# Layer 0's second shift on VectorE in the last two branches, the scale alone on TensorE, and the gate's row behind two row tiles of the output projection

## The chip, the cores and the metric

The kernel runs on one core of one Trainium2 chip. Its engines are TensorE (PE in the rows; PEld is its weight load), VectorE (DVE), ScalarE (ACT), GpSimd (POOL) and SyncE (SP, which here issues nearly all DMAs). The metric is the device time of one execution in microseconds (us), as the median of several runs, lower being better.

## The reference, cut to what matters

One inference step of a two-layer network over 256 latent and 128 context tokens, D = 1024. Each layer is a token-mixing sub-layer and a channel mixer, both wrapped in a modulation and a gate that depend on two condition vectors, one for each token group (v = 0 context, v = 1 latent):

```python
sh1, sc1, g1, sh2, sc2, g2 = split(silu(c) @ w_mod[l] + b_mod[l], 6)
h = layer_norm(x) * (1 + sc1) + sh1
...  # attention, convolution and Fourier branches, merged by three sigmoid gates
x = layer_norm(ALPHA * x + g1 * (merged @ w_o)) * ln1_g + ln1_b
h = layer_norm(x) * (1 + sc2) + sh2
...  # up projection, depthwise conv of 3, silu gate, down projection
x = layer_norm(ALPHA * x + g2 * (... @ w_down)) * ln2_g + ln2_b
```

The six vectors of 1024 that `w_mod` gives are read by the kernel in three pairs: "A" is (sh1, sc1), "B" is (sh2, sc2), "G" is (g1, g2), with j = 0 or 1 for the member of the pair. The change deals with where B of layer 0 is computed, and with when g1 is made ready for use.

## The kernel before

**Products.** Activations are kept transposed (features on partitions, 384 tokens in the free dimension). Each weight tile of 128x1024 is split into a high part (`whi`, a cast on ScalarE, L183) and a low part (`wlo`, a subtraction on VectorE, L184); each product is then three matmuls (`mm3`, L200, L201, L202). The pools are small: 3 `raw` tiles of 1 MB, 5 `whi`, 5 `wlo`, 8 `s4` tiles of 512 KB, 8 `s2` tiles of 256 KB, and in PSUM 2 `ps` and 6 `acc` tiles.

**Token mixing** (`mixing`, L624) computes the projections, then three branches in turn, each over eight 128-row tiles m: Fourier (branch 0, with the attention's `scores` and `values` and the depthwise convolution `conv_branch` spread over it), attention output (branch 1) and convolution output (branch 2). For each m a branch does a gate product of 24 matmuls (L666), tanh on ScalarE (L669), an output product (12 matmuls in branch 1, 6 in branches 0 and 2), a merge on VectorE (L683) and an addition on GpSimd (L684). In branch 2 the merged tile is split again for the next product (`split`, ScalarE L652, VectorE L653).

**The attention's values** (`values`, L873): for each head of a pair, seven transposes, a ScalarE copy of 512 columns (L884) and a VectorE copy of 384 columns (L885) from PSUM, then the products L893 and L896.

**Modulation has two ways.** On TensorE, `mod_stream` (L252) brings 8 tiles of 512 columns a step (two k of four quarters each, `STRIDE` = 2), multiplies them in `mod_products` (L221, 32 rows of PSUM a quarter), and after the last k `mod_columns` copies the sums, transposes them in four blocks (L301) and adds the bias. Before, layer 0 does the whole pair B so, in four steps; each instruction of L221 shows as two records in the trace, so the 32 instructions of the pair are 64 records. On VectorE, `mod_rows` (L311) multiplies a row-major 512 KB tile of `w_modr` by a broadcast condition vector and sums along the row, for both v (L331, two instructions for a tile, eight tiles for one vector of 1024, called a unit here). `paced` (L357) spreads the units' tiles over a number of calls: before, in each layer's mixing one unit (g1) over 10 calls, from tile m = 4 of branch 1 on.

**The gate's row** (`gate_rows`, L346): the unit's sums are transposed on TensorE (L351), copied by ScalarE (L353) and written to a scratch in HBM (L354), from which `gate_bc` (L370) reads them back to all partitions, 512 KB for each v. Before, this stands at the end of `mixing` (L736); `layer` (L971) then asks for the gate and the layer norm's vectors and starts the output projection, four loads of `w_o` with two row tiles k each. The first three k are multiplied for all tokens, the last five (`TAIL`) token tile by token tile, so that the closing of tile 0 (`close`, L943 on) can begin early. `close` multiplies each half by the gate first.

**Order.** The program text gives the order of priorities; the framework fixes each engine's queue when it builds, so an instruction can stand ahead of its place in the text, but each queue then runs strictly in that order. `issue_after` pins an instruction behind a given one.

Of the kernel before, what the change touches and what calls it, by code (L numbers as in the profile page):

```python
# [77 lines left out]
class Net:  # L78
# [135 lines left out]
    STRIDE = 2  # L214
# [37 lines left out]
    def mod_stream(self, groups):  # L252


        steps = [(l, kind, k) for l, kind in groups for k in range(0, KD, self.STRIDE)]
        src = {}

        def fetch(l, kind, k0):
            for k in range(k0, k0 + self.STRIDE):
                w = self.a["w_mod"][l, self.MODS[kind], k].rearrange("p j (i c) -> p (j i) c", c=512)  # L260
                for i in range(4):
                    src[k, i] = self.s2()
                    self.load(src[k, i], w[:, i])

        fetch(*steps[0])
        yield
        for n, (l, kind, k0) in enumerate(steps):
            if k0 == 0:
                ps = self.psum("acc")
            self.mod_products(ps, src, range(k0, k0 + self.STRIDE), 512)  # L270
            if k0 + self.STRIDE == KD:
                if kind == "G":
                    self.mod_gates(l, ps)
                else:
                    self.mod_columns(l, kind, ps, 512, 0, "acc")
            if n + 1 < len(steps):
                fetch(*steps[n + 1])
            yield

    def mod_gates(self, l, ps):  # L280
        nc, a, n = self.nc, self.a, 512
        row = self.s2()
        nc.gpsimd.memset(row, 0.0)
        r4 = row.rearrange("(j i r) c -> j i r c", r=32, j=2)
        for v in range(2):
            for j in range(2):
                self.load(r4[j, :, v, :], a["b_g"][l, j].rearrange("(i c) -> i c", c=n))
        nc.vector.tensor_tensor(row, ps, row, op=ALU.add)
        for v in range(2):
            for j in range(2):  # L290
                nc.sync.dma_start(self.gscr[l, j, v].rearrange("(i c) -> i c", c=n), r4[j, :, v, :])
# [54 lines left out]
    def gate_rows(self, tag):  # L346

        nc = self.nc
        for l, j, cols in self.gate_sums:
            pt = self.psum(tag)[0:2 * KD, 0:P]  # L350
            nc.tensor.transpose(pt, cols, self.ident)  # L351
            row = self.kk()[0:2 * KD, :]
            nc.scalar.copy(row, pt)  # L353
            nc.sync.dma_start(self.gscr[l, j].rearrange("v (k p) -> (v k) p", p=P), row)  # L354
        self.gate_sums = []
# [268 lines left out]
    def mixing(self, l, first, hT, mods, rows):  # L624
# [69 lines left out]
        mods = self.mod_stream(mods) if mods else iter(())  # L694
# [4 lines left out]
        step_rows = self.paced(rows, 10)  # L699
# [24 lines left out]
        for i, _ in enumerate(branch(1, 0, "w_a", 4, aT, lambda: values(3))):  # L724
            next(cb, None)
            if i >= 4:
                step_rows()
            if i % 2:
                mod()
# [6 lines left out]
        self.gate_rows("acc")  # L736
# [77 lines left out]
    def attention(self, l, z, cv, out):  # L814
# [58 lines left out]
        def values(j):  # L873
            pT = []
            for par in range(2):
# [9 lines left out]
                nc.vector.tensor_copy(p[:, 512:896], pts[1][:, 0:384])  # L885
# [85 lines left out]
    def layer(self, l, first, hT, mods, mix_rows, rows):  # L971
        nc, a = self.nc, self.a
        m_hl = self.mixing(l, first, hT, mods, mix_rows)
        gate = self.gate_bc(l, 0)
        lg, lb = self.bcast(a["ln"][l, 0]), self.bcast(a["ln"][l, 1])
# [3 lines left out]
        for u in range(KD // 2):  # L979
            for h, w in enumerate(self.row_halves(self.raw(a["w_o"][l, u]))):  # L980
                k = 2 * u + h
                if k < KD - self.TAIL:
                    self.x_mm(acc, k, KD, m_hl[k], w, range(3), off)
                else:
                    held.append((k, w))

# [146 lines left out]
    def run(self):  # L1133
        self.setup()
        xhat = [self.s4() for _ in range(3)]
        mods = [[(0, "B")], []]
        mix_rows = [[(0, "G", 0)], [(1, "G", 0)]]
# [83 lines left out]
```

## Time and profile before

| | |
|---|---|
| median of 3 runs | 1136.67 us (1135.53 to 1137.31) |
| the profiled execution | 1136.51 us, of which the span is 1134.6 us |
| granted TensorE clock | 0.998 of full speed |
| TensorE / VectorE / ScalarE / GpSimd busy | 98% / 78% / 46% / 8% |

Layer 0's mixing runs from about 60 to 254 us of the span, its output projection to 273 us; layer 1's mixing ends at 804 us. Branch 0 is under way at 100 us in layer 0 and at 657 us in layer 1. The rows below are taken from the profile's page and from views of the trace.

### The profile page before, as it was taken

What the parts mean: (1) busy time and instruction counts of PE and PEld (TensorE: products, weight loads), DVE (VectorE), ACT (ScalarE), POOL (GpSimd) and SP (SyncE); (2) the same over time, 40 slices, a digit from 0 to 9 for tenths busy, and PEclk for the clock granted to TensorE, in tenths of its full rate; (3) what the DMA queues carried; (4) which work ended last, traced back from release to release, by engine and by line L of the source; (5) the groups of instructions that cost most, each with busy time, mean ns of one, the idle gap of its engine ahead of it and who ended that gap; (6) DMA issues with size and microseconds to landing.
All of it is one profiled execution on the core that took longest, in us unless ns stands there. A gap on an engine that the chain in (4) does not pass through costs nothing.

```text
span 1134.6 us, 16426 instructions
## 1 busy us (share of the span) xinstructions
PE 1116.2 (98%) x6385; PEld 1014.7 (89%) x6385; DVE 888.2 (78%) x1519; ACT 521.8 (46%) x879; POOL 89.5 (8%) x89
## 2 busy tenths in 40 slices
PE   9999999999999999999999999999999999999996
PEld 7788889998999998999957989999889999999995
DVE  6579968856899999999776699796579975556668
ACT  3457744342754343443363686334356343444440
POOL 1010003221100000000011000222120000000001
PEclk9999999999999999999999999999999999999999
DMA  9863563636566666658335222564626543434511
GB/s 377 309 214 130 168 240 117 218 111 223 186 223 222 217 212 217 238 177 294 113 112 185 96 75 75 191 217 149 231 92 253 194 141 117 144 111 158 176 38 55
DMA packets 41821, 199.04 MB, mean 175 GB/s; under 512 B 4912, under 2 KB 6032, under 8 KB 26640
## 3 DMA queue, kind: packets, MB, share of 16 engines
q1 hardware_dynamic: 41312, 197.21, 49.8%
q8 instruction: 50, 0.82, 0.3%
q10 hardware_dynamic: 432, 0.79, 0.2%
q14 instruction: 27, 0.22, 0.1%
HBM read 194.53 MB, written 3.45 MB: 174 GB/s over the span
## 4 chain that ended last, share of the span: by engine, by line
PE 83%; DVE 10%; ACT 2%; issue 2%; POOL 1%; DMA 1%; POOLq 0%; DVEq 0%; ACTq 0%
PE ps L200 16%; PE ps L202 16%; PE ps L201 16%; PE acc L200 9%; PE acc L201 9%; PE acc L202 9%; DVE wlo L184 1%; PE acc L893 1%; DVE s L331 1%; DVE sm L425 1%; DVE s L944 1%; POOL sm L429 1%; PE acc L129 1%; PE acc L881 1%; DMA s<-w_modr 1%
## 5 line engine op out<-in xcount | busy, mean ns | idle before, releaser
L184 DVE TENSOR_TENSOR wlo<-raw,whi 128x1024 fp32r<-128x1024 f32 x216 | 269.4, 1252 | 145.1 <-ACT whi L183 141.2
L200 PE MATMUL ps<-hT,whi 128*128 128x386 f32 (+1 forms) x1088 | 370.3, 340 | 2.4 <-ACT g L669 1.5
L202 PE MATMUL ps<-hT,wlo 128*128 128x386 f32 (+1 forms) x1088 | 368.9, 339 | 0.0
L201 PE MATMUL ps<-hT,whi 128*128 128x386 f32 (+1 forms) x1088 | 368.6, 339 | 0.0
L183 ACT CAST whi<-raw 128x1024 fp32r<-128x1024 f32 x216 | 225.9, 1050 | 309.8 <-PE ps L201 183.0
L200 PEld LDWEIGHTS ps<-hT,whi 128*128 128x128 f32 x1088 | 205.3, 189 | 9.0 <-issue 3.3
L201 PEld LDWEIGHTS ps<-hT,whi 128*128 128x128 f32 x1088 | 205.4, 189 | 1.5 <-issue 0.4
L202 PEld LDWEIGHTS ps<-hT,wlo 128*128 128x128 f32 x1088 | 205.5, 189 | 0.8 <-issue 0.7
L331 DVE SCALAR_TENSOR_TENSOR s<-s,s 128x1024 f32<-128x1024 f32 x128 | 160.8, 1256 | 5.0 <-DMA s<-w_modr 4.5
L201 PE MATMUL acc<-wlo,r 128*128 128x512 f32 x360 | 142.4, 396 | 0.9 <-DVE wlo L184 0.9
L202 PE MATMUL acc<-whi,r 128*128 128x512 f32 x360 | 141.9, 394 | 0.0
L200 PE MATMUL acc<-whi,r 128*128 128x512 f32 x360 | 140.4, 395 | 0.0
L202 PEld LDWEIGHTS acc<-whi,r 128*128 128x128 f32 x360 | 67.7, 188 | 15.8 <-DVE r L1077 0.5
L201 PEld LDWEIGHTS acc<-wlo,r 128*128 128x128 f32 x360 | 67.7, 188 | 15.5 <-DVE wlo L184 1.3
L200 PEld LDWEIGHTS acc<-whi,r 128*128 128x128 f32 x360 | 67.7, 188 | 14.7
L429 POOL TENSOR_TENSOR sm<-sm,mhalf 128x1 f32<-128x1 f32 x21 | 26.8, 1274 | 625.2 <-DVE sm L428 625.2
L911 DVE SCALAR_TENSOR_TENSOR cv<-upad,cst,cv 128x399 f32<-128x399 f32 x120 | 70.6, 633 | 0.1
L684 POOL TENSOR_TENSOR g<-g,g 128x384 f32<-128x384 f32 x32 | 45.1, 1409 | 322.6 <-DVE g L683 322.6
L1053 ACT ACTIVATE g<-ps,cst 128x386 f32<-128x386 f32 x84 | 56.1, 667 | 0.0
L1054 DVE SCALAR_TENSOR_TENSOR g<-ps,cst,g 128x385 f32<-128x385 f32 x84 | 51.6, 614 | 2.5 <-ACT g L1053 2.4
L1056 DVE SCALAR_TENSOR_TENSOR g<-ps,cst,g 128x385 f32<-128x385 f32 x84 | 51.9, 618 | 1.3
L1076 ACT CAST r<-g 128x386 fp32r<-128x386 f32 x44 | 22.6, 514 | 65.8 <-DVE g L1074 65.8
(194 smaller groups left out, 1318.5 us busy)
## 6 DMA issues: line engine op xcount, KB each, us to landing
raw<-w_u SPq DMA_DIRECT2D x44, 1024.0 KB, 4.9
s<-w_modr SPq DMA_DIRECT2D x64, 512.0 KB, 3.6
raw<-w_g SPq DMA_DIRECT2D x24, 1024.0 KB, 5.0
raw<-w_d SPq DMA_DIRECT2D x22, 1024.0 KB, 4.9
raw<-w_mod SPq DMA_DIRECT2D x8, 1024.0 KB, 8.6
s<-w_mod SPq DMA_DIRECT2D x32, 256.0 KB, 4.6
raw<-w_o SPq DMA_DIRECT2D x8, 1024.0 KB, 4.9
s<-w_z SPq DMA_DIRECT2D x8, 512.0 KB, 9.8
```

Of the source, the lines that this page charges most:

```text
L183: self.nc.scalar.copy(hi, raw)
L184: self.nc.vector.tensor_tensor(lo, raw, f32(hi), op=ALU.subtract)
L200: mm(ps, lh, rh, start=first, stop=False)
L201: mm(ps, lh, rl, start=False, stop=False)
L202: self.last_mm = mm(ps, ll, rh, start=False, stop=last)
L331: nc.vector.scalar_tensor_tensor(prod, w[i % 2], 1.0, cb[v], op0=ALU.mult, op1=ALU.mult, accum_out=sums[n][:, v * KD + k:v * KD + k + 1])
L429: nc.gpsimd.tensor_tensor(mv[:, 3:4], mv[:, 2:3], self.mhalf, op=ALU.pow)
L684: nc.gpsimd.tensor_tensor(merged[m], merged[m], gt, op=ALU.add)
L911: nc.vector.scalar_tensor_tensor(c, u[:, i:i + CV_W], w, c, op0=ALU.mult, op1=ALU.add)
L1053: nc.scalar.activation(c, ps, AF.Identity, bias=cols["ffn_b"][:, i:i + 1], scale=w[1])
L1054: nc.vector.scalar_tensor_tensor(c[:, 1:NPAD], ps[:, 0:NPAD - 1], w[0], c[:, 1:NPAD], op0=ALU.mult, op1=ALU.add)
L1056: nc.vector.scalar_tensor_tensor(c[:, 0:NPAD - 1], ps[:, 1:NPAD], w[2], c[:, 0:NPAD - 1], op0=ALU.mult, op1=ALU.add)
```

## The change

`mod_stream` now computes only the scale of B (j = 1), for the layer it is given; `mod_columns` stays for nothing but what the first projection does by itself. A step takes four k (`STRIDE` = 4) of 1024 columns: again 8 tiles of 512 columns, each of which holds two quarters of 256, so there are two steps and 32 instructions of 256 columns; `mod_column` makes two transposes, not four. The shift of B (j = 0) becomes a unit of layer 0's mixing beside g1, so there are two units there, over 14 calls from tile m = 2 of branch 1 on. Layer 1 keeps one unit over 10 calls. The VectorE copy in `values` goes to ScalarE in both layers. `gate_rows` moves, in both layers, from the end of `mixing` to behind the first load of the output projection (two k), takes a `ps` tile instead of an `acc` tile, and its transpose is pinned behind the last matmul of those two k; the loads of the gate and the layer norm's vectors stand behind all of `w_o`'s in the text. `mod_gates`, which nothing called, is gone.

```diff
-    STRIDE = 2
+    STRIDE = 4
...
-    def mod_stream(self, groups):
-        steps = [(l, kind, k) for l, kind in groups for k in range(0, KD, self.STRIDE)]
+    def mod_stream(self, l):
         src = {}
-        def fetch(l, kind, k0):
+        def fetch(k0):
             for k in range(k0, k0 + self.STRIDE):
-                w = self.a["w_mod"][l, self.MODS[kind], k].rearrange("p j (i c) -> p (j i) c", c=512)
-                for i in range(4):
-                    src[k, i] = self.s2()
-                    self.load(src[k, i], w[:, i])
+                w = self.a["w_mod"][l, self.MODS["B"], k, :, 1]
+                for h in range(2):
+                    t = self.s2()
+                    self.load(t, w[:, h * 512:h * 512 + 512])
+                    for i in range(2):
+                        src[k, 2 * h + i] = t[:, i * 256:i * 256 + 256]
...
-            self.mod_products(ps, src, range(k0, k0 + self.STRIDE), 512)
+            self.mod_products(ps, src, range(k0, k0 + self.STRIDE), 256)
...
+    def mod_column(self, l, j, ps):
+        nc = self.nc
+        row = self.s2()[:, 0:256]
+        nc.vector.tensor_copy(row, ps[:, 0:256])
+        pt = self.psum("acc")
+        for q in range(2):
+            nc.tensor.transpose(pt[:, q * P:(q + 1) * P], row[:, q * P:(q + 1) * P], self.ident)
+        bias = self.bmod[l][:, j + 3, :].rearrange("p (i q) -> p i q", q=2)
         for v in range(2):
+            part = pt[:, 0:256].rearrange("p (q i r) -> p r i q", q=2, i=4)[:, v]
+            dst = self.modcol[l][:, j + 2, v, :].rearrange("p (i q) -> p i q", q=2)
+            nc.vector.tensor_tensor(dst, part, bias, op=ALU.add)
...
-    def gate_rows(self, tag):
+    def gate_rows(self, tag, after=None):
...
-            nc.tensor.transpose(pt, cols, self.ident)
+            if after:
+                with self.tc.issue_after(after):
+                    nc.tensor.transpose(pt, cols, self.ident)
+            else:
+                nc.tensor.transpose(pt, cols, self.ident)
...
-        step_rows = self.paced(rows, 10)
+        step_rows = self.paced(rows, 14 if len(rows) > 1 else 10)
...
-            if i >= 4:
+            if i >= (2 if len(rows) > 1 else 4):
                 step_rows()
...
-        self.gate_rows("acc")
         return m_hl
...
-                nc.vector.tensor_copy(p[:, 512:896], pts[1][:, 0:384])
+                nc.scalar.copy(p[:, 512:896], pts[1][:, 0:384])
...
         m_hl = self.mixing(l, first, hT, mods, mix_rows)
-        gate = self.gate_bc(l, 0)
-        lg, lb = self.bcast(a["ln"][l, 0]), self.bcast(a["ln"][l, 1])
...
+            if u == 0:
+                self.gate_rows("ps", self.last_mm.ins)
+        gate = self.gate_bc(l, 0)
+        lg, lb = self.bcast(a["ln"][l, 0]), self.bcast(a["ln"][l, 1])
...
-        mods = [[(0, "B")], []]
-        mix_rows = [[(0, "G", 0)], [(1, "G", 0)]]
+        mods = [True, False]
+        mix_rows = [[(0, "B", 0), (0, "G", 0)], [(1, "G", 0)]]
```

## Rows read from the trace of the kernel before

**Rows 1.** Page, part 1; stages: length, engines (PE to POOL), clock, DMA share, GB/s.

```profile
PE 1116.2 (98%) x6385; PEld 1014.7 (89%) x6385; DVE 888.2 (78%) x1519; ACT 521.8 (46%) x879; POOL 89.5 (8%) x89
...
103.00:157.00 54.00, 54.00 (x352) 44.24 (x351) 50.85 (x113) 36.14 (x88) 0.00 (x0) 1.00 0.54 184
...
165.00:182.00 17.00, 17.00 (x101) 16.96 (x100) 8.55 (x16) 4.17 (x6) 3.56 (x4) 1.00 0.42 157
182.00:222.00 40.00, 40.00 (x232) 39.82 (x231) 37.33 (x57) 15.34 (x21) 12.63 (x7) 1.00 0.56 184
222.00:255.00 33.00, 33.00 (x190) 32.74 (x188) 17.41 (x25) 15.29 (x24) 8.20 (x7) 1.00 0.39 128
255.00:270.00 15.00, 15.00 (x66) 12.20 (x65) 7.33 (x9) 4.23 (x5) 1.20 (x1) 1.00 0.87 311
```

**Rows 2.** The chain of waits, modulation products (start, us, what).

```profile
43.46 1.88 PE ps L221 x64
...
118.95 1.85 PE acc L221 x16
...
157.52 0.44 PE acc L301 x4
```

**Rows 3.** The same columns, between the same instructions of layers 0 and 1.

```profile
100.19:179.11 78.92, 78.89 (x501) 67.21 (x502) 63.87 (x137) 45.93 (x103) 2.04 (x2) 1.00 0.57 197
657.26:729.19 71.93, 71.93 (x433) 65.48 (x434) 63.74 (x132) 45.84 (x103) 2.94 (x2) 1.00 0.36 128
```

**Rows 4.** Groups of instructions by line: copies, row sums; weight loads' waits.

```profile
L331 DVE SCALAR_TENSOR_TENSOR s<-s,s 128x1024 f32<-128x1024 f32 x128 | 160.8, 1256 | 5.0 <-DMA s<-w_modr 4.5
L884 ACT COPY s<-acc 128x512 f32<-128x512 f32 x16 | 8.9, 579 | 2.5 <-PE acc L881 2.5
L885 DVE COPY s<-acc 128x384 f32<-128x384 f32 x16 | 8.8, 552 | 3.0 <-PE acc L882 2.8
L761 ACT COPY g<-acc 128x256 f32<-128x256 f32 x8 | 3.4, 428 | 0.0
...
PEld acc L893 <- ACT s L884: 2.4, 7, 0.8
PEld acc L893 <- DVE s L885: 1.1, 2, 0.8
```

**Rows 5.** The last two branches in order of time, on VectorE, TensorE and GpSimd.

```profile
218.12 1.22 DVE L184 TENSOR_TENSOR wlo<-raw,whi 128x1024 fp32r<-128x1024 f32 x1
219.25 2.04 DVE L331 SCALAR_TENSOR_TENSOR s<-s,s 128x1024 f32<-128x1024 f32 x1
...
222.56 0.55 DVE L683 SCALAR_TENSOR_TENSOR g<-g,acc 128x384 f32<-128x384 f32 x1
...
226.92 0.55 DVE L683 SCALAR_TENSOR_TENSOR g<-g,acc 128x384 f32<-128x384 f32 x1
...
230.34 1.22 DVE L184 TENSOR_TENSOR wlo<-raw,whi 128x1024 fp32r<-128x1024 f32 x1 [2.40 <-ACT whi L183]
...
217.01 0.34 PE L202 MATMUL acc<-r,wlo 128*128 128x384 f32 x1
...
222.27 0.34 PE L202 MATMUL acc<-r,wlo 128*128 128x384 f32 x1
...
227.61 1.20 POOL L684 TENSOR_TENSOR g<-g,g 128x384 f32<-128x384 f32 x1 [3.36 <-DVE g L683]
```

**Rows 6.** The gate's row and the first closing in order of time; its DMAs.

```profile
253.96 0.27 PE L351 MATMUL acc<-ident,sm 128*16 128x128 f32 x1
...
254.62 0.33 SPq L354 DMA_DIRECT2D gscr<-kk  x1
...
256.71 0.80 SPq L122 DMA_DIRECT2D s<-gscr  x2
...
270.27 0.69 DVE L943 TENSOR_TENSOR s<-acc,s 128x512 f32<-128x512 f32 x1 [1.18 <-PE acc L202]
...
DMA to landing us min/median/max: 2.0/7.2/8.1
```

More of the change, by code (lines that the diff above doesn't have):

```diff
@@ L250, in mod_first @@
         yield
-    def mod_stream(self, groups):
-        steps = [(l, kind, k) for l, kind in groups for k in range(0, KD, self.STRIDE)]
+    def mod_stream(self, l):
         src = {}
-        def fetch(l, kind, k0):
+        def fetch(k0):
             for k in range(k0, k0 + self.STRIDE):
-                w = self.a["w_mod"][l, self.MODS[kind], k].rearrange("p j (i c) -> p (j i) c", c=512)
-                for i in range(4):
-                    src[k, i] = self.s2()
-                    self.load(src[k, i], w[:, i])
-        fetch(*steps[0])
+                w = self.a["w_mod"][l, self.MODS["B"], k, :, 1]
[4 more added lines that the diff above has]
+                        src[k, 2 * h + i] = t[:, i * 256:i * 256 + 256]
+        fetch(0)
@@ L266, in mod_stream @@
         yield
-        for n, (l, kind, k0) in enumerate(steps):
+        for k0 in range(0, KD, self.STRIDE):
             if k0 == 0:
                 ps = self.psum("acc")
-            self.mod_products(ps, src, range(k0, k0 + self.STRIDE), 512)
+            self.mod_products(ps, src, range(k0, k0 + self.STRIDE), 256)
             if k0 + self.STRIDE == KD:
[L272 to L277, printed above, removed]
-            yield
@@ L280, in mod_gates @@
[L280 to L284, printed above, removed]
-        for v in range(2):
[L286 to L291, printed above, removed]
+                self.mod_column(l, 1, ps)
+            else:
+                fetch(k0 + self.STRIDE)
@@ L350, in gate_rows @@
             pt = self.psum(tag)[0:2 * KD, 0:P]
-            nc.tensor.transpose(pt, cols, self.ident)
+            if after:
+                with self.tc.issue_after(after):
+                    nc.tensor.transpose(pt, cols, self.ident)
+            else:
+                nc.tensor.transpose(pt, cols, self.ident)
             row = self.kk()[0:2 * KD, :]
@@ L693, in mixing @@
             self.columns(l + 1, self.columns_load(l + 1), nc.vector.tensor_copy)()
-        mods = self.mod_stream(mods) if mods else iter(())
+        mods = self.mod_stream(l) if mods else iter(())
         def mod():
             next(mods, None)
-        step_rows = self.paced(rows, 10)
+        step_rows = self.paced(rows, 14 if len(rows) > 1 else 10)
         ci = conv_in()
```

## The prediction, made before the change was run

> **What bounds the kernel now.** I read the page first, for the busy shares, then busy time by stage, the chain of waits, and single engines in order of time. TensorE is busy 98% of the span [rows 1]; in the stages of layer 0's mixing it is busy for 54.00 of 54, 40.00 of 40 and 33.00 of 33 us. The reader should see that VectorE comes second and unevenly: 50.85 of 54 us beside the attention, 8.55 of 17 at the start of branch 1, 37.33 of 40 while the row sums run, 17.41 of 33 after them. So an instruction taken from TensorE in the mixing can shorten the run, and work given to VectorE is free only where it finds those idle stretches: 17 - 8.55, 40 - 37.33 and 33 - 17.41, together 26.7 us.
>
> **The modulation on TensorE.** Before, 64 records of 512 columns. Sixteen take 1.85 us [rows 2], so 64 take 7.4. After, 64 records of 256 columns, a width the trace does not have. The neighbours bound it: 64 records of 128 columns took 1.88 us, so the new ones take between 1.88 and 7.4 us. A straight line in the columns gives 1.88 + (7.4 - 1.88) / 3 = 3.7, and I take it, since both ends are the same instruction with the same weight load. That removes 3.7 us (between 0 and 5.5). Four transposes took 0.44 us; two fewer save 0.2. Together 3.9 us of TensorE's time.
>
> What of it reaches the end? Layer 1 has the same attention without this modulation. Between the same two instructions, the first matmul after the wait for tanh and the convolution's transposes L919, layer 0 needs 78.92 us and layer 1 needs 71.93 [rows 3]: 7.0 us apart, for 7.4 + 0.44 = 7.84 us of TensorE's work. The share that counts is 0.89, the rest fills waits. So 3.9 us are worth **3.5 us** on the path.
>
> Beside the attention, TensorE's weight load is busy 44.24 of 54 us and in the last branches 39.82 of 40 [rows 1]. The Trainium skill (Trainium Kernel Development and Optimization, Performance Expectations) says that matmul busy time is a bad measure of how close TensorE is to its limit and weight load busy time a good one. By 44.24 / 54 = 0.82 the gain would be 3.9 x 0.82 = 3.2 us, not 3.5, and by the comparison of the layers 3.5; no row shows which part of the gap is a wait.
>
> The loads of a step stay eight of 256 KB, two steps instead of four; the eight row-major tiles of 512 KB that come instead are the same 4 MB, in a later stage whose DMA share is 0.42 to 0.56 [rows 1]. On VectorE the copy of the sums shrinks and two small additions go: nothing, since the result is wanted only in the channel mixer; there is no cover to lose.
>
> **The copies moved to ScalarE.** Sixteen copies of 0.552 us leave VectorE, 8.8 us in both layers [rows 4]. ScalarE's price for 384 columns lies between its 256-column copy, 0.428 us, and its 512-column copy, 0.579; I take 0.5. ScalarE is busy 36.14 of 54 us there, so room is no question; the order is. Each head's two copies ran side by side on two engines and now stand in line, so the products behind them can be up to 0.5 us later, eight times: at most 4.0 us. At best the wait of 1.1 us that weight loads had for the VectorE copy vanishes. I take +0.2, near the better end, because other products are queued between the transposes and the products of a pair, and VectorE's copy was itself late. Cover gone, it costs rival 1.
>
> **The shift as row sums.** Eight tiles, two instructions each at 1.256 us [rows 4]: 16 x 1.256 = 20.1 us, and some meet GpSimd's addition and take 2.04 instead of about 1.22 [rows 5]. Three of 16 did so before; three more make 2.5, so 22.6 us of VectorE for 26.7 us of idle time, which leaves 4.1. The work fits, with a lag. Before, the lag was already there: the product of tile 0 of branch 2 ended at 217.01 + 0.34, its merge on VectorE began at 222.56, 5.2 us late; one tile on it was 226.92 against 222.61, 4.3 late [rows 5]. TensorE did not wait, since the low weights were ahead: the ones written from 218.12 to 219.34 served the product that began at about 222.6, 3.3 us of margin, and the next ones have more. The sums now begin about two tiles earlier, where VectorE is half idle, and go on in branch 2, where it waits 2.40 us an iteration for the cast on ScalarE, almost the length of one tile's two sums (2.5). What is queued behind a sum is the next low weights, the merge, and through GpSimd and ScalarE the next split. SP's queue holds the fetches of row-major tiles, which wait for the sums to free a buffer, ahead of weight loads; with three 1 MB tiles and the DMA share above I cost that at nothing, and if that cover is gone the weights come as late as in rival 3. Bounds: 0 (margin holds) to 5.8 us (rival 3). I take **+0.6**, as the lag before cost nothing at 5.2 us.
>
> The meetings with GpSimd are a case of a rule: by the Trainium skill (SBUF — State Buffer, Who interferes with whom) a VectorE instruction with two SBUF inputs and a GpSimd instruction that reads SBUF exclude each other, and the second blocks fully. By it a meeting would cost up to GpSimd's 1.20 us, 3.6 for three; the rows show 2.04 - 1.22 = 0.82, and the sum goes by that.
>
> **The gate's row.** Its transpose leaves the start of the output projection and comes two k later: 253.96 [rows 6] plus 36 matmuls, which in the stage from 255 to 270 are spaced 15 / 66 = 0.23 us [rows 1], that is near 262.3. The scratch write followed 0.66 us behind, the first read 2.09 us after that, so the reads would be issued near 265.1 and 265.5. They landed 7.2 and 8.1 us after issue before, in a stretch with a DMA share of 0.87 that also carried the layer norm's vectors, `x` and up weights; these need no gate and can now go ahead of it. The gate is wanted at 270.27, and harmless until about 271.6: the second half's product ends 15 matmuls or 3.5 us later, and the first half has three instructions of 0.69 to do until then, 2.1. A read that takes below 6 us is in time. I cost the move at 0; its ScalarE copy, one scratch write and two reads a layer stay the same count, but SP's queue waits at the write, and up weights and `x` behind it wait with it. The `ps` tile it takes is wanted next by the up projection, much later. The gain of the move, nothing late at 254, is 0 too: TensorE was full up to 255 [rows 1]. Bounds: 0 to 2.0 us a layer.
>
> **Sum.** -3.5 + 0.2 + 0.6 + 0 = -2.7 us, from the profiled execution's 1136.51 (span 1134.6 and 1.9 around it): **1133.8**. That execution is 0.16 below the median of the runs. About 0.2%, 2.3 us, is what a measurement here can tell from no change.
>
> **Rivals.**
> 1. *Copies in line.* The eight pairs of copies hold the attention's products by the full 0.5 us, less the 1.1 that vanishes: +2.9 in place of +0.2, giving 1136.5, no change. For it: weight loads waited 2.4 us for the ScalarE copy already [rows 4]. Against: those waits were short, at most 0.8, with other products between.
> 2. *The gate late in both layers.* Reads that take 7.2 to 8.1 us as before come at 272.3 to 273.6, 0.7 to 2.0 past 271.6, say 1.5 in each layer: +3.0, giving 1136.8, no change. For it: the write is waited for in SP's queue. Against: half of what shared the DMA engines can go first.
> 3. *VectorE's round becomes the bound, and it is slower.* In branch 2 each merge waits for low weights, these for the cast, the cast for the split, the split for GpSimd's addition, which waits for the merge before: a round of 226.92 - 222.56 = 4.4 us against TensorE's 222.27 - 217.01 = 5.3 [rows 5]. If a tile's two sums stand in series with it, not in the gap of 2.40, the round is 4.4 + 2.5 = 6.9, 1.6 us more than TensorE's; over the eight tiles 13 us, less about 7 of margin that low weights have by tile 6 (3.3 at tile 2, and 0.9 more with each tile, as the lag shrank from 5.2 to 4.3): 5.8 us, in place of 0.6. That gives 1139.0, slower. It decides as soon as the lag passes the margin, where branch 1 turns into branch 2. For it: 22.6 of 26.7 us. Against: work in the gap costs the round almost nothing.
>
> **How the numbers follow.** The forecast has 0.53, rival 1 has 0.12, rival 2 has 0.19, rival 3 has 0.16. So faster 0.53, same 0.31, slower 0.16. The best of the bounds together, 3.5 + 1.1 and the new records 0.7 nearer to the price of 128 columns, is 5.3 below the profiled execution: 1131.2. The range reaches from there to rival 3, 1139.2. The forecast's own range is 1131.2 to 1134.3.
>
> **What would show it.** Right: between the same two instructions of rows 3, layer 0 shrinks by 3 to 4 us and layer 1 hardly changes; the 64 records cover 3.7 us; VectorE is above 90% busy through the last two branches and TensorE still full; the first merge multiplication by the gate waits for the product, not for the read. Wrong: weight loads of L893 waiting longer for L884 and its new neighbour (rival 1); L943 waiting for a DMA (rival 2); weight loads or matmuls of the branches waiting for the low weights, L184, or for a free `acc` tile (rival 3).

## The result and the profile after

The changed kernel takes 1147.6 us (median of 4 runs, 1146.5 to 1148.23) against 1136.52 for the kernel before (1135.53 to 1137.31): ratio 1.0092, 95% interval 1.0080 to 1.0104. It is **slower by 11 us**, where 1133.8 was predicted. The profiled execution has a span of 1145.9 us against 1134.6, 11.3 more.

The page of the changed kernel, part 1, answers to the first line of [rows 1]:

```profile
PE 1117.0 (97%) x6383; PEld 1014.4 (89%) x6383; DVE 901.8 (79%) x1535; ACT 527.4 (46%) x895; POOL 88.7 (8%) x89
```

The changed kernel's busy time by stage, with the columns of [rows 1] (length, PE, PEld, DVE, ACT, POOL, granted clock, DMA share, GB/s); the last two stretches are parts of the one above them:

```profile
165.00:182.00 17.00, 17.00 (x101) 16.96 (x101) 10.07 (x19) 5.36 (x7) 5.44 (x6) 1.00 0.44 169
182.00:222.00 40.00, 40.00 (x232) 39.81 (x231) 39.31 (x57) 14.16 (x21) 12.25 (x7) 1.00 0.66 221
222.00:255.00 33.00, 32.11 (x178) 30.91 (x177) 32.35 (x46) 12.55 (x19) 5.98 (x5) 1.00 0.55 185
255.00:270.00 15.00, 10.73 (x37) 8.22 (x38) 9.28 (x15) 5.54 (x8) 2.38 (x2) 0.77 0.55 197
255.70:260.20 4.50, 0.96 (x3) 0.48 (x3) 3.17 (x7) 2.87 (x4) 1.19 (x1) 0.75 0.28 118
260.20:264.70 4.50, 4.46 (x11) 3.50 (x12) 4.13 (x5) 1.46 (x2) 1.19 (x1) 0.50 0.71 233
```

The busy shares hardly move; the stages tell it. VectorE is busy for 32.35 of 33 us in branch 2, where it had 17.41 before, and TensorE, full before, is busy for 10.73 of 15 us from 255 to 270, with a granted clock of 0.77.

To see where the 11 us come in, I set the start of an instruction after against the start of the same one before. The offset is -0.3 us at 100 us, ahead of all that was changed, and -3.1 at the convolution's transposes (near 179 us); on TensorE and ScalarE it stays so until 217. In branch 2 tanh on ScalarE slips from -3.1 to +4.5 at the last row tile. TensorE slips much less there: it is still at -2.4 when it begins the output projection, and most of its loss falls behind that point. The first closing's second half is at +5.0 and its statistics at +7.7, layer 1's mixing runs at about +9.9 from end to end, and layer 1's output projection and closing take it to +11.3. So five things are to be explained: a gain kept until 217 us, a lag in branch 2 that TensorE pays for at the output projection, a loss at the first closing, some 2 us between that and layer 1's mixing, and a small loss in layer 1.

**Branch 2.** The changed kernel in order of time, VectorE and then ScalarE (L329 is a row sum, L685 the merge, L654 and L655 the split):

```profile
225.32 0.55 DVE L685 SCALAR_TENSOR_TENSOR g<-g,acc 128x384 f32<-128x384 f32 x1
225.78 0.55 DVE L655 SCALAR_TENSOR_TENSOR r<-g,r 128x384 fp32r<-128x384 f32 x1
226.25 2.04 DVE L329 SCALAR_TENSOR_TENSOR s<-s,s 128x1024 f32<-128x1024 f32 x1
228.33 1.23 DVE L329 SCALAR_TENSOR_TENSOR s<-s,s 128x1024 f32<-128x1024 f32 x1
229.60 1.23 DVE L329 SCALAR_TENSOR_TENSOR s<-s,s 128x1024 f32<-128x1024 f32 x1
230.75 0.55 DVE L685 SCALAR_TENSOR_TENSOR g<-g,acc 128x384 f32<-128x384 f32 x1
...
221.94 0.53 ACT L654 ACTIVATE r<-g 128x384 fp32r<-128x384 f32 x1 [7.28 <-POOL g L686]
223.32 0.57 ACT L671 ACTIVATE g<-ps,cst 128x384 f32<-128x384 f32 x1
227.24 0.53 ACT L654 ACTIVATE r<-g 128x384 fp32r<-128x384 f32 x1 [3.36 <-POOL g L686]
...
257.00 0.52 ACT L654 ACTIVATE r<-g 128x384 fp32r<-128x384 f32 x1 [4.43 <-POOL g L686]
258.37 0.57 ACT L671 ACTIVATE g<-ps,cst 128x384 f32<-128x384 f32 x1
```

Three row sums stand between the two merges shown; in the other rounds it is two or three. ScalarE shows what that holds up: its queue has the split of tile m - 1, a cast, then tanh, and the split waits for GpSimd's addition, which waits for the merge. From the first split shown to the last are six rounds, (257.00 - 221.94) / 6 = 5.84 us each; before, the same seven splits ran from 224.29 to 251.83, 4.59 a round. TensorE's tile takes 5.3 us [rows 5]. The round was shorter than TensorE's and caught up; now it is longer and falls behind with every tile. TensorE itself meets this only once in branch 2, in a wait of 0.4 us for tanh (in the table of waits below). Idle time is used up: with its `DVE_READ_ACCUMULATOR` records the sums take 43.37 us from 178 to 256, against 22.07 before, 21.3 more, and VectorE idles for 1.8 us in the 77.3 from 178.9 on.

**The output projection.** TensorE of the changed kernel in order of time:

```profile
251.60 0.39 PE L200 MATMUL acc<-whi,r 128*128 128x512 f32 x1
251.84 0.39 PE L201 MATMUL acc<-wlo,r 128*128 128x512 f32 x1
...
255.69 0.51 PE L200 MATMUL acc<-whi,r 128*128 128x512 f32 x1 [1.14 <-DVE g L685]
256.04 0.39 PE L201 MATMUL acc<-wlo,r 128*128 128x512 f32 x1
...
260.24 0.80 PE L200 MATMUL acc<-whi,r 128*128 128x512 f32 x1 [3.57 <-DVE g L685]
...
261.26 0.63 PE L202 MATMUL acc<-whi,r 128*128 128x512 f32 x1
261.68 0.63 PE L200 MATMUL acc<-whi,r 128*128 128x512 f32 x1
...
264.67 0.44 PE L201 MATMUL acc<-wlo,r 128*128 128x512 f32 x1
```

From its table of waits, 150 to 300 us (total us, times, longest); the second line is the wait for tanh in branch 2:

```profile
PE acc L200 <- DVE g L685: 4.7, 2, 3.6
...
PE ps L200 <- ACT g L671: 0.4, 1, 0.4
```

TensorE is early when it begins (251.60), but `acc` tiles that it wants still hold branch 2's last products, which no merge has taken. It waits 1.14 and 3.57 us. Behind the longer wait matmuls stand 0.43 us apart, not 0.23, and the granted clock of 260.20 to 264.70 above is 0.50, that is 1.2 in place of 2.4 GHz: ten intervals take 4.43 us in place of 2.3. From 254.16 to 264.67, with the waits, the half clock and the slower first matmuls, TensorE loses 7.3 us and goes from -2.4 to +4.9.

**The first closing.** SP's queue and then VectorE of the changed kernel, to be read against [rows 6]; L944 multiplies by the gate, L945 adds `x`, L429 ends the statistics:

```profile
268.75 0.32 SPq L356 DMA_DIRECT2D gscr<-kk  x1
271.32 0.82 SPq L122 DMA_DIRECT2D s<-gscr  x2
272.19 0.90 SPq L122 DMA_DIRECT2D s<-ln  x2
273.13 0.70 SPq L122 DMA_DIRECT2D s<-x_s  x1
...
276.79 0.69 DVE L944 TENSOR_TENSOR s<-acc,s 128x512 f32<-128x512 f32 x1 [2.74 <-DMA s<-gscr]
278.73 0.69 DVE L944 TENSOR_TENSOR s<-acc,s 128x512 f32<-128x512 f32 x1 [1.24 <-PE acc L202]
281.13 1.29 DVE L945 SCALAR_TENSOR_TENSOR s<-s,s 128x512 f32<-128x512 f32 x2 [1.72 <-DMA s<-x_s]
...
283.66 0.21 DVE L429 BATCH_NORM_AGGREGATE sm<-sm 128x2 f32<-128x12 f32 x1
```

The layer norm's vectors and `x` were issued at 257.57 and 261.17 before; now they stand behind the scratch write in SP's queue and go out at 272.19 and 273.13. L944 waits for the gate, but the second half waits for the product in any case; what then holds the closing is `x`: both halves' additions come behind it, 1.72 us after VectorE has done that multiplication.

**What TensorE gained.** The modulation's records now, by the view of one line:

```profile
L221 PE MATMUL acc<-s,cpad x64: 379/379/403, 103.2 to 121.9; 128*32 128x256 f32 x64
```

They cover 4.28 us, against 8.11 for the 64 records of 512 columns in the same view. Between the two instructions of [rows 3] layer 0 now needs 2.8 us less (the first starts at 99.93, the transposes at 175.97, against 100.19 and 179.06 before), and layer 1 0.1 more.

### The profile page after: what moved, and what is told of

It reads as the page before. It is cut to its first block, busy times and chain, and to the rows that moved or that the text cites. A ratio compares the mean times of both kernels' runs of the same rounds, so it can differ in the third digit from the quotient of the medians.

```text
span 1145.9 us, 16454 instructions
## 1 busy us (share of the span) xinstructions
PE 1117.0 (97%) x6383; PEld 1014.4 (89%) x6383; DVE 901.8 (79%) x1535; ACT 527.4 (46%) x895; POOL 88.7 (8%) x89
## 4 chain that ended last, share of the span: by engine, by line
PE 61%; DVE 6%; ACT 2%; issue 2%; DMA 1%; POOL 1%; POOLq 0%; DVEq 0%; ACTq 0%
PE ps L200 13%; PE ps L202 13%; PE ps L201 12%; PE acc L202 6%; PE acc L200 6%; PE acc L201 6%; DVE s L329 1%; DVE wlo L184 1%; PE acc L894 1%; PE ps L1029 1%; PE acc L1029 1%; PE acc L1122 1%; DMA raw<-w_d 1%; ACT whi L183 1%; DVE s L955 0%
## 5 line engine op out<-in xcount | busy, mean ns | idle before, releaser
L329 DVE SCALAR_TENSOR_TENSOR s<-s,s 128x1024 f32<-128x1024 f32 x144 | 182.1, 1265 | 8.0 <-ACT s L469 5.2
L431 POOL TENSOR_TENSOR sm<-sm,mhalf 128x1 f32<-128x1 f32 x21 | 26.8, 1275 | 626.3 <-DVE sm L430 361.0
L1079 ACT CAST r<-g 128x386 fp32r<-128x386 f32 x44 | 22.6, 514 | 62.6 <-DVE g L1077 62.5
```

Source lines behind the costliest of these rows:

```text
L329: nc.vector.scalar_tensor_tensor(prod, w[i % 2], 1.0, cb[v], op0=ALU.mult, op1=ALU.mult, accum_out=sums[n][:, v * KD + k:v * KD + k + 1])
L431: nc.gpsimd.tensor_tensor(mv[:, 3:4], mv[:, 2:3], self.mhalf, op=ALU.pow)
```

## The experiments

Two views do most of the work in what follows: offsets of the same instruction as above, and the table of waits. An offset at a time in the mixing or beside the output projection is that of tanh on ScalarE, unless TensorE is named. The edits are cut; those of gate_alone and copies_alone are against the kernel before, the others against the kernel that the text names or, where a line of the change is taken back, against the changed kernel. Each time is the median of its runs with the ratio to the kernel before, measured on the same chip.

| kernel | us | ratio, 95% interval |
|---|---|---|
| gate_alone | 1142.98 | 1.0057 (1.0037 to 1.0077) |
| copies_alone | 1138.82 | 1.0012 (1.0003 to 1.0022) |
| shift_alone | 1142.77 | 1.0047 (1.0032 to 1.0062) |
| no_copies | 1149.26 | 1.0107 (1.0087 to 1.0127) |
| sums_left_out | 1135.71 | 0.9991 (0.9981 to 1.0000) |
| gate_sums_first | 1142.88 | 1.0051 (1.0036 to 1.0066) |
| sums_early | 1139.34 | 1.0020 (1.0010 to 1.0029) |
| gate_ln_x_first | 1137.63 | 1.0006 (0.9997 to 1.0015) |
| no_shift_g1_early | 1134.47 | 0.9975 (0.9965 to 0.9985) |
| after_loads_first | 1144.80 | 1.0067 (1.0053 to 1.0081) |
| sums_tail | 1140.63 | 1.0026 (1.0015 to 1.0036) |
| sums_planned | 1136.31 | 0.9994 (0.9985 to 1.0003) |

### One part at a time

**gate_alone**: the kernel before with `gate_rows` and the loads behind it moved as in the change, and nothing else.

```diff
-        self.gate_rows("acc")
         return m_hl
...
-        gate = self.gate_bc(l, 0)
-        lg, lb = self.bcast(a["ln"][l, 0]), self.bcast(a["ln"][l, 1])
...
+            if u == 0:
+                self.gate_rows("ps", self.last_mm.ins)
+        gate = self.gate_bc(l, 0)
+        lg, lb = self.bcast(a["ln"][l, 0]), self.bcast(a["ln"][l, 1])
```

> The kernel before with one part of the change: the gate's row and the gate's loads behind the first two k of the output projection, in both layers; the modulation and the copies as before. Theory A (the gate comes late by its own place): the first multiplication by the gate waits for the read of the scratch by 1 to 3 us in each layer, and the time is 2 to 5 us above before (1138.5 to 1141.5). Theory B (the gate is late only because VectorE's row sums lag): no wait for the scratch, time within 0.8 us of before.

It has about half of the whole change's loss. The scratch write is issued at 263.32, the reads at 266.48, vectors and `x` at 267.34 and 268.29. The offset is -0.4 us through layer 0's mixing, +2.7 behind its first closing, +3.1 in layer 1's mixing and +4.6 behind layer 1's closing. The closing, with line numbers of this kernel (L946 by the gate, L947 adds `x`, L431 ends the statistics):

```profile
271.79 0.69 DVE L946 TENSOR_TENSOR s<-acc,s 128x512 f32<-128x512 f32 x1 [3.12 <-DMA s<-gscr]
273.34 0.69 DVE L946 TENSOR_TENSOR s<-acc,s 128x512 f32<-128x512 f32 x1 [0.86 <-PE acc L202]
276.11 1.29 DVE L947 SCALAR_TENSOR_TENSOR s<-s,s 128x512 f32<-128x512 f32 x2 [2.08 <-DMA s<-x_s]
...
278.64 0.21 DVE L431 BATCH_NORM_AGGREGATE sm<-sm 128x2 f32<-128x12 f32 x1
```

The expected wait for the gate is there, 3.12 us, but so is one that was not: 2.08 us for `x`. Which of the two costs is not settled by this run; gate_ln_x_first, below, does that.

**copies_alone**: the kernel before with the one copy moved.

```diff
-                nc.vector.tensor_copy(p[:, 512:896], pts[1][:, 0:384])
+                nc.scalar.copy(p[:, 512:896], pts[1][:, 0:384])
```

> The kernel before with one part of the change: the 384-column copy of the attention on ScalarE. Theory A and B alike (the copies play no part): within 0.8 us of before. Rival C (copies in line hold the products): 2 to 3 us above before, with longer waits of the weight loads of the attention's products for ScalarE.

The loss is 1.2 us of the span, and it comes in layer 0's attention: between the two instructions of [rows 3] it needs 1.9 us more (offset +1.0 at 129 us, +1.6 at 172), layer 1's 0.1 more, and 0.4 come back in layer 0's channel mixer. The copy takes 0.487 us on ScalarE (median). Small, and above the forecast's 0.2.

**shift_alone**: the scale alone on TensorE and the shift as a unit of row sums over 14 calls, with the gate's row and the copies as before. The edit is against the changed kernel; the gate's loads go back to their old place as well.

```diff
+        self.gate_rows("acc")
         return m_hl
...
-                nc.scalar.copy(p[:, 512:896], pts[1][:, 0:384])
+                nc.vector.tensor_copy(p[:, 512:896], pts[1][:, 0:384])
```

> The kernel before with one part of the change: the scale alone on TensorE and the shift as row sums, 14 calls from tile 2 of branch 1; the gate's row stays at the end of the mixing, the copies on VectorE. Theory V (VectorE's lag is the larger loss): the output projection cannot start at its time, since accumulators are held by products that VectorE has not merged and the gate's transpose waits for the last sums; TensorE idles 4 to 8 us between 250 and 262 and the time is 3 to 8 us above before (1139.5 to 1144.5). Theory A (only the gate's new place costs): 1133 to 1134, 3 us below before.

The offsets are those of the whole change in the mixing: -3.2 until 217 us, -1.7, +1.7 and +5.2 at 226, 239 and 254. It arrives at the closing with +5.8. TensorE is at -1.7 when the mixing ends, and the longest wait is that of the gate's transpose, the first instruction behind it, for the last of the row sums:

```profile
PE acc L353 <- DVE sm L339: 5.3, 1, 5.3
```

**no_copies**: the whole change with the copy back on VectorE (the second hunk above).

> The changed kernel with the copies of the attention back on VectorE. If the copies play no part: within 1 us of the changed kernel (1146.5 to 1148.5). If they cost (rival C): 2 to 3 us below it. If they relieve VectorE in the stage where it lags: 1 to 3 us above it.

Its interval overlaps that of the whole change, and the traces say the same more sharply: between the two instructions of [rows 3] layer 0 shrinks by 2.7 us here and by 2.8 in the changed kernel. With the scale alone on TensorE the moved copies cost nothing there. The loss of copies_alone is found only in the attention that has the whole pair B in it; layer 1's, without modulation, lost 0.1. Why, no run shows.

The three parts measured alone give ratios that add up to 1.0116, against 1.0092 for the change; the intervals are too wide to make much of the difference. The gate's row and the shift are two separate losses, in different stages. That of the copies is not there in the changed kernel.

### Why the shift costs

**sums_left_out**: shift_alone, with the shift's fetches and queue places but without its sums.

```diff
-            for v in range(2):
+            for v in range(0 if len(units) == 2 and units[n][1] == "B" else 2):
                 nc.vector.scalar_tensor_tensor(prod, w[i % 2], 1.0, cb[v], ...
```

> The scale alone on TensorE, the gate's row and the copies as before, and the shift's unit of two with its fetches, its places in the queues and its bias, but without its 16 row sums (the shift's product with the condition is left out: the sums are set to zero). Theory C (the sums' own time on VectorE turns the shift into a loss): TensorE's gain of 3.0 us is kept to the end, 1132.5 to 1134.5, no matmul waits over 1 us between 245 and 260 us, and the granted clock stays at 1.00 there. Rival D (the eight extra fetches of 512 KB, or the longer lag of SP's queue, hold the weights): still over 1138.

The loss is gone, so the sums make it and not the fetches by themselves; and in the changed kernel no cast of branches 1 and 2 (178 to 262 us) waits for a weight. But only 1 us of the 3 is gained (1.4 in the profile), and that was expected by neither side. The offset of tanh is -3.3 at 217 us and -1.0 at 226. TensorE loses less than that: it waits once, goes from -3.3 to -2.3, and keeps that until the closing; 0.9 more go between there and layer 1's mixing. So "2.3 of TensorE's 3.3 us were lost", in the expectation of no_shift_g1_early below, is the slip of tanh and not that of TensorE, which was 1.0. The chain of waits of this kernel at that place (start, us, what; L332 a sum, L688 the merge, L689 GpSimd's addition, L674 tanh):

```profile
217.19 0.21 DVE s L332
...
219.60 1.14 DVE wlo L184
220.74 0.48 DVE g L688
221.34 1.88 POOL g L689
...
223.68 1.03 ACT whi L183
224.71 0.49 ACT g L674
225.24 0.45 PE ps L200
```

The wait at its end, and then the same place in the kernel before, where the product at 227.69 takes the `ps` tile that this tanh frees:

```profile
225.24 0.45 PE L200 MATMUL ps<-hT,whi 128*128 128x384 f32 x1 [0.71 <-ACT g L674]
...
225.66 0.57 ACT L669 ACTIVATE g<-ps,cst 128x384 f32<-128x384 f32 x1
227.69 0.34 PE L200 MATMUL ps<-hT,whi 128*128 128x384 f32 x1
```

The sum at 217.19 is one of g1's, which the kernel before has as well. A merge behind it, the addition, the split and the cast on ScalarE, tanh, and then TensorE, which waits for tanh to free its `ps` tile. In the kernel before tanh ends 1.5 us ahead of that product (227.69 - 226.23): that was the slack here. With tanh itself 1.0 us earlier, TensorE could keep 2.3 of the 3.3 us by which it came early, and the rest went into the wait.

**gate_sums_first**: shift_alone with the units in the other order.

```diff
-        mix_rows = [[(0, "B", 0), (0, "G", 0)], [(1, "G", 0)]]
+        mix_rows = [[(0, "G", 0), (0, "B", 0)], [(1, "G", 0)]]
```

> Shift alone with the two units in the other order: g1's tiles first, the shift's behind. Theory E (of the loss of 5.6 us, the gate's transpose waiting 5.3 us for the last sums is the main part): the transpose no longer waits, 1136 to 1139. Rival F (VectorE has fallen behind by its whole work, so the merges hold the accumulators in any order): matmuls into acc wait for L685 instead, as long as in the changed kernel (3 to 5 us), the clock falls to half behind that wait, and the time stays within 1.5 us of shift alone, 1141.3 to 1144.3.

Theory E falls. The transpose is in time, yet its ScalarE copy is behind the late splits (TensorE waits 2.5 us for the accumulator that it holds) and the merges hold another for 1.7 us; offset +6.0 at 254 us, and TensorE at +6.5 behind it. Rival F's size holds, with the wait split over two causes: the lag itself is what has to go.

**no_shift_g1_early**: no shift unit at all, and g1's over its 10 calls from tile 2, not 4.

```diff
-        mix_rows = [[(0, "B", 0), (0, "G", 0)], [(1, "G", 0)]]
+        mix_rows = [[(0, "G", 0)], [(1, "G", 0)]]
...
-            if i >= (2 if len(rows) > 1 else 4):
+            if i >= (2 if l == 0 else 4):
```

> The scale alone on TensorE, no shift unit at all, neither sums nor fetches (the shift's product with the condition is left out, its bias alone stands), and g1's unit over its 10 calls from tile 2 of branch 1 on, not from tile 4. Theory J (in sums_left_out 2.3 of TensorE's 3.3 us were lost where branch 2 begins, since the first merge there was behind g1's own row sums, and tanh behind its split on ScalarE): with g1's sums two tiles earlier the first split comes in time, no product waits for L671's tanh at branch 2's start, and the gain stays 2.5 to 3.3 us to layer 0's closing; 1133 to 1134.5. Rival K (something else, such as the loads of weights, sets branch 2's start): the offset falls to about 1 us there again, 1135 to 1136.

Theory J holds. No wait of TensorE is left between 150 and 300 us, the offset is -3.1 to -3.2 from 172 us to the closing and -2.5 in layer 1, and the time is 0.9975 of before. With VectorE's sums out of the way at branch 2's start, TensorE's gain reaches the closing, 0.8 us more of it than in sums_left_out.

### Why the gate's row costs

**gate_ln_x_first**: gate_alone, with the vectors and the first tile of `x` loaded ahead of the output projection's weights.

```diff
+        lg, lb = self.bcast(a["ln"][l, 0]), self.bcast(a["ln"][l, 1])
+        x0 = self.s4()
+        self.load(x0, self.x_src(l, 0))
         acc = [[self.psum("acc"), self.psum("acc")] for _ in range(3)]
...
         gate = self.gate_bc(l, 0)
-        lg, lb = self.bcast(a["ln"][l, 0]), self.bcast(a["ln"][l, 1])
```

> Gate alone, with the layer norm's two vectors and the first tile of x loaded before the output projection's weights, so that only the gate's own reads stand behind the scratch write in SP's queue. Theory H (half of the loss is that these loads stand behind a write that waits): the multiplication by x no longer waits for a DMA (2.1 us in gate alone), the reads of the gate land a little sooner for want of company; loss against before falls from 4.6 to 5.8 us to 1 to 3: 1138 to 1140. Rival I (the gate's reads alone set the closing's start): the wait for gscr stays at 3.1 us or more and the time at 1141.5 to 1143.

```profile
271.74 0.69 DVE L946 TENSOR_TENSOR s<-acc,s 128x512 f32<-128x512 f32 x1 [3.11 <-DMA s<-gscr]
272.47 0.69 DVE L947 SCALAR_TENSOR_TENSOR s<-s,s 128x512 f32<-128x512 f32 x1
...
273.81 0.67 DVE L946 TENSOR_TENSOR s<-acc,s 128x512 f32<-128x512 f32 x1
...
275.97 0.21 DVE L431 BATCH_NORM_AGGREGATE sm<-sm 128x2 f32<-128x12 f32 x1
```

The time is that of the kernel before (the profiled execution is 2.2 us longer, all of it behind the closing, where its offset is 0.0). The wait for the gate is the same 3.1 us as in gate_alone, as rival I said, and it costs nothing: the second half starts 0.1 us off its time before, since the first half is done by then, and the statistics end at 275.97, not at 278.64. So it was not the gate that came too late but the loads that queue behind its write.

**after_loads_first**: the whole change with that same edit.

> The whole change, with the layer norm's two vectors and the first tile of x loaded before the output projection's weights, as in gate_ln_x_first. Theory H (the gate's share of the loss is these loads standing behind the scratch write): 3.5 to 5 us of the 11 come back, 1142.5 to 1144.5, and the multiplication by x waits for no DMA. Rival L (with VectorE and TensorE late, the gate's own reads are late too and set the closing): less than 2 us come back, 1145.5 or more, with the first multiplication by the gate and the product's second half waiting behind gscr.

The result lies between the two expectations: 1.0092 becomes 1.0067, 2.8 us. The closing no longer waits for `x`, but L944's wait of 2.3 us for the gate stays, and its second half is at +6.7: what the shift costs is untouched by this edit. TensorE even comes 1.8 us later here than in the changed kernel (+6.7 against +4.9, for which no run gives a cause), and so less comes back than theory H expected.

### Can both gains be had?

**sums_early**: gate_sums_first with 16 calls from tile 0 of branch 1 on.

```diff
-        step_rows = self.paced(rows, 14 if len(rows) > 1 else 10)
+        step_rows = self.paced(rows, 16 if len(rows) > 1 else 10)
...
-            if i >= (2 if len(rows) > 1 else 4):
+            if i >= (0 if len(rows) > 1 else 4):
```

> As gate_sums_first, but the 17 steps of the two units are spread over 16 calls, from tile 0 of branch 1 on, so that the idle time of VectorE at branch 1's start (8.45 of 17 us before) is used. Theory C (what counts is that VectorE's queue has no room between 179 and 256): sums end some 3 us earlier, the lag at the end of branch 2 shrinks to below what the six accumulators cover, 1134 to 1137. Rival G (the early sums delay the attention's last pair and the conv's steps on VectorE, and so the output product of branch 1): loss of 1 us or more against before already by tile 2 of branch 1, 1138 or more.

Some of each. More than half of shift_alone's loss is gone, but 2.3 us of TensorE's gain are lost at the convolution's transposes (here L929, from -3.1 to -0.8), as rival G said. A sum of 1.91 us at 177.71 and two more behind it went in between the instructions of the norm, and the table of waits has the longest wait that follows:

```profile
PE acc L929 <- DVE g L436: 1.6, 1, 1.6
```

**sums_tail**: three of the shift's tiles beside the output projection, pinned behind the last merge, with g1 first and the loads early.

```diff
+        step_rows = self.paced(rows, 18 if len(rows) > 1 else 10)
...
             for n in range(2):
                 tail(t, n)
+                with self.tc.issue_after(self.last_merge):
+                    more_rows()
```

> A version meant to keep both gains: scale alone on TensorE, copies and gate's row as before, g1's tiles first and the shift's behind, over 18 calls of which the last four stand in the output projection behind the last merge (three of the shift's tiles there), the gate in four half tiles, the vectors and the first x loaded early. Theory C (VectorE's lag in branch 2 is the loss; the shift is not needed before the channel mixer): branch 2's last four merges find VectorE free, no wait for accumulators at the output projection, and the gain of up to 3 us is kept in part: 1134 to 1136.5. Rival M (the sums beside the output projection hold its low weights, or the lag at branch 2's start costs as before): 1138 or more.

Rival M: no wait for a merge is left, but the lag of tanh at 226 to 244 us is still there (+1.6 at 244), and TensorE waits 2.7 us for the output projection's last low weight, which stands behind the six sums (the fifth of these itself waits 1.18 us for its fetch).

**sums_planned**: sums_tail with the calls written out, each behind its own tile's merge.

```diff
-        step_rows = self.paced(rows, 18 if len(rows) > 1 else 10)
+        todo = self.mod_rows(rows)
+        plan = iter([2, 1, 0, 1, 1, 1, 1, 1, 0, 1, 1, 1, 1, 1, 1, 1, 1, 1, 0, 0])
...
+                    with self.tc.issue_after(self.last_merge):
+                        next(todo, None)
```

> A second version meant to beat both kernels, from what sums_early and sums_tail lost: scale alone on TensorE, copies and gate's row as before (a ps tile for its transpose), g1's tiles first. The 16 tiles of the two units by a written plan, each behind the merge of its own row tile: two behind branch 1's first two merges, where VectorE idles, none beside the convolution's norm, five in the rest of branch 1, none behind branch 2's first merge, seven in branch 2, two in the output projection. Theory C (what costs is a sum that stands ahead of a merge, of the conv's norm or of a low weight): the offset stays at -3 us to 217 us, no wait of over 1 us from 178 to 250, 1134 to 1136.5. Rival N (VectorE simply has not room for 20 us more before the closing, in any order): 16 sums fill branch 2 as before, TensorE or the closing waits 2 us or more there, 1137 to 1140.

Theory C holds in the mixing: the offset is -3.2 us at 217, TensorE keeps it to the mixing's end, and it waits for nothing from 178 to 250. One wait is left beside the output projection,

```profile
PE acc L201 <- DVE wlo L184: 1.3, 1, 1.3
```

the closing is at -1.7, and about 2 us go on the way from there to layer 1 (+0.3). The time is that of the kernel before within what can be told. Against no_shift_g1_early the shift's eight tiles, 16 sums, now cost 1.9 thousandths, some 2.2 us, where shift_alone pays 7.2 thousandths, 8.2 us, for the same work. Pacing alone is worth 3.1 thousandths, 3.5 us (gate_sums_first against sums_early). The rest is not shown part by part: this version has another order again, but also the vectors and the first `x` early, the gate in half tiles and two tiles of sums beside the output projection. No version that I ran with the shift's sums on VectorE beats the kernel before.

The last 2 us go in layer 0's channel mixer. From the closing to layer 1's mixing between 0.6 and 2.1 us go in every kernel with the scale alone on TensorE, but 1.9 in gate_ln_x_first too, so that part of the change is not needed for it. In sums_planned's table of waits from 280 to 640 us TensorE waits for VectorE to free a `ps` tile of the up projection, three times and 1.4 us in all, where it waited once, 0.7 us, in the kernel before, and 0.9 us longer for ScalarE. Why VectorE and ScalarE are late there is open; no run took it apart.

## Why the prediction was wrong

**TensorE's gain: there, but smaller.** 3.5 us on the path were predicted. Between the two instructions of [rows 3] layer 0 shrinks by 2.7 to 2.8 us in every run with the scale alone on TensorE, less than the 3 to 4 named as a sign. (The offsets of about -3.1 hold some 0.3 to 0.4 us more that were there at 100 us; gate_ln_x_first has 0.45 too, with nothing changed up to there.) The work was right: the records cover 3.83 us less (8.11 - 4.28), where 3.7 was estimated. What was too high is the share that counts: about 0.7 (2.8 of 3.83 and the 0.2 taken for the transposes), not the 0.89 read from layer 1. The Trainium skill (Trainium Kernel Development and Optimization, Performance Expectations) takes weight load busy time as the better measure; the estimate of 3.2 us made with it is nearer, but the trace does not give it either.

**The shift as row sums: the step that failed first.** The price of the sums was right (21.3 us of VectorE where 22.6 was worked out, into 26.7 of idle time), and so was the place, where branch 1 turns into branch 2. What failed is "I take +0.6, as the lag before cost nothing at 5.2 us". A lag that costs nothing says that there is slack, not how much: tanh had 1.5 us left in the kernel before, and sums_left_out shows that TensorE's gain alone, without one sum more, spends it. The margin that I worked out was that of the low weights. The path that decides is another: merge, GpSimd's addition, the split on ScalarE, and tanh queued behind the split. Its round grew from 4.59 to 5.84 us, past TensorE's 5.3. TensorE pays little of that in branch 2 (0.4 us of waits in the changed kernel, 0.8 in shift_alone) and most of it where the mixing ends: the output projection wants `acc` tiles that no merge has freed, or (in shift_alone) the gate's transpose wants the last sum. Rival 3 said that the round decides, with a round of 6.9 and a loss of 5.8, but put the wait on the low weights; measured, the loss is what shift_alone gives back and adds, 3.2 + 5.8 = 9.0 us at the closing. Part of it is the half clock behind the wait, 2.0 us there, which no rival had.

**The gate's row: the second step that failed.** "These need no gate and can now go ahead of it" was an assumption on the order of SP's queue, taken neither from a row nor from the text of the change, which puts the loads of the gate and of the vectors in this order behind `w_o`'s, and `x` behind them. They go behind the write. "Harmless until about 271.6" was right: the gate came at 271.7 and cost nothing once the loads were ahead. Rival 2 had the size (+3.0, where the profile of gate_alone shows 4.7 and its runs 5.8) with the wrong cause.

**The copies: right for the change, by luck.** +0.2 was taken. Alone they cost 1.2 us of the span, 1.9 of it at first in layer 0's attention; in the changed kernel they cost nothing (no_copies). Neither the reason given for +0.2 nor rival 1 has such a difference in it.

**What would show it.** Two of the signs named for the rivals were there: the first multiplication by the gate waits for a DMA, and matmuls wait for `acc` tiles. VectorE above 90% through the last two branches was named for the forecast; from 182 us on it came, and it was the trouble.

**The range.** I priced the rivals one against the other. They sit in different stages, so they add: by their own prices, 1133.8 + 2.7 + 3.0 + 5.2 = 1144.7, far outside a range that ended at the largest of them alone (at 1139.2, where rival 3's own sum gives 1139.0). That it comes near the 1147.6 measured is partly luck: the copies' 2.7 was not there, and the other two cost more than their price.

## What to carry to other kernels

When an edit speeds up the engine that sets the pace, the slack of every other engine shrinks by up to that much; read that slack at the tile that is waited for, or measure it by leaving the added work out, and do not infer it from a lag that happens to be free. Take offsets on the engine that sets the pace: here tanh slipped by 2.3 us where TensorE lost 1.0. Work given to an engine with idle time is priced by what is queued behind it, and so by where in the queue it stands: pacing alone took 3.5 us off, and the same eight tiles of sums cost 8.2 us when spread evenly and 2.2 in the version with each tile of the mixing behind a merge. When a write that waits for an engine is moved later in a queue, everything that follows it there moves too: list those loads by name, and put what needs no wait in front.

## What I had not expected of the hardware

The long waits on TensorE here cost more than their length. Behind 3.57 us the granted clock is 0.50 for 4.5 us and matmuls stand 0.43 us apart; in shift_alone, behind 5.29 us, they stand so for 4.4 us, with a granted clock of 0.50 from 257.70 to 262.10. Behind the wait of 1.14 us at 255.69 the spacing is back at 0.23 with the second matmul. The Trainium skill (TensorE: Matmul & The Clock Gate, What's actually happening) describes the two levels, 1.2 and 2.4 GHz. These rows show what the fall costs here, some 2 us on top of each of the two long waits.
